# Loads of half a buffer, and two stores divided by rows into 112, 12 and 4, in an RMSNorm-matmul kernel

## The chip, the cores and the metric

The kernel runs on one core of one Trainium2 chip. The metric is the device time of one execution in microseconds (us), lower is better. A run counts as slow when it lies more than 1.5 per cent above the fastest run of the same kernel; verdicts use the others, the fast runs. The *span* of a profile is shorter than the time, by 1.8 us in the profiled run of the kernel before (208.8 and 210.53).

## The reference, cut to what matters

```python
# x [16, 1024, 512], gamma [512], weight [512, 768], all float32
rms = np.sqrt(np.mean(x ** 2, axis=-1, keepdims=True) + eps)
x_norm = x / rms * gamma
return np.matmul(x_norm, weight).astype(np.float32)      # [16, 1024, 768]
```

That is 16,384 tokens in 128 tiles of 128. The kernel reads 35 MB and writes 50 MB, so 85.5 MB have to pass through the DMA engines.

## The kernel before

A load brings 16 tiles: 128 rows, one for each partition of the on-chip memory, with 16 tokens of 2,048 B, that is 32,768 B a row. There are two such buffers. A store writes 8 tiles, 128 rows of 24,576 B, from one of three output buffers. All run on the sync engine's DMA queue. `XG` is 16, `OG` is 8, `NT` 128, `P` 128.

```python
    x_first, x_size = stretches(XG, {0: [2, 2, 4, 8], 1: [8, 8]})        # how each buffer is loaded
    o_first, o_size = stretches(OG, {0: [2, 2, 4], 1: [4, 4], last: [4, 4]})
    xin = ctx.enter_context(tc.tile_pool(name="xin", bufs=2))
    outp = ctx.enter_context(tc.tile_pool(name="out", bufs=3))
    ...
    def load(i):
        if i // XG not in x_tiles:
            x_tiles[i // XG] = xin.tile([P, XG, D], F32, name="xt")
        nc.sync.dma_start(out=held(x_tiles, XG, i, x_size[i]), in_=rows(x, i, x_size[i]))
    ...
    def store(i):
        first, n = o_first[i], o_size[i]
        if i == first + n - 1:
            nc.sync.dma_start(out=rows(out, first, n), in_=held(o_tiles, OG, first, n))
    ...
        marks = {NP - 10: (12, 13, 14, 15)}         # near the end: tiny loads of 12, 13, 14, 15 rows
        for j in range(1, NP):                      # a pair of tiles
            load_until(2 * j + AHEAD)
            ...                                     # GpSimd: cast to bf16; VectorE or TensorE: transpose
            for i, engine in ((2 * j, nc.scalar), (2 * j + 1, nc.vector)):
                a = accumulator()
                matmuls(i, a, range(K), feed)       # TensorE
                finish_tile(i, a, engine)           # scale by 1/rms into the output buffer, store
```

## Time and profile before

| | before |
|---|---|
| time, first three runs | 210.05, 210.16, 210.49 us |
| span of the profile | 208.8 us |
| TensorE busy | 195.0 us |
| bytes moved, rate over the span | 85.69 MB, 410 GB/s |
| last store: issued, first and last engine landed | 200.46, 206.46, 207.86 us |

The landings come from the steps of the DMA semaphores in the trace, one step read as one engine whose share has landed (a whole store shows 16 steps, the marks of 12 to 15 rows show 12 to 15). A *packet* is one row of a transfer on one DMA engine, 24,576 B in a whole store. The *granted clock* is the share of full speed that TensorE was given.

### The profile page before, as it was taken

The page shows a single profiled execution, that of the slowest core. Times are in us where ns is not written, and L with a number is a line of the kernel's source. Part 1 is how long each engine was busy: PE and PEld are TensorE (multiplying, and loading weights), DVE is VectorE, ACT ScalarE, POOL GpSimd, SP SyncE. Part 2 cuts the span into 40 slices and gives each one's busy share as a digit, 9 for nine tenths or more (in the row PEclk, how much of TensorE's full clock was granted, in tenths as well). Part 3 has the DMA queues.
Part 4 walks back from the last instruction along what each step waited for, and adds up shares of the span by engine and source line. Part 5 has one row for each costly group of instructions (what it writes and reads, how often), then busy time and mean ns, then how long its engine had stood idle before and what let it go on. Part 6 is the DMA issues. An engine that isn't in the chain of part 4 may idle for free.

```text
span 208.8 us, 3466 instructions
## 1 busy us (share of the span) xinstructions
PE 195.0 (93%) x1238; PEld 129.3 (62%) x1238; DVE 150.9 (72%) x270; ACT 149.6 (72%) x358; POOL 64.3 (31%) x65
## 2 busy tenths in 40 slices
PE   7799999999999999999999999999999989999910
PEld 2367767665677666666766666665667646666600
DVE  0465657997399957998499957998489955999410
ACT  4698787778677887788777877788678768778310
POOL 3247535003910193004810086001930049000000
PEclk9999999999999999999999999999999999999995
DMA  6999999999999999999999999999999999994994
GB/s 240 429 436 440 358 391 432 472 403 432 421 436 425 421 438 416 465 377 436 414 455 438 403 430 433 440 427 421 435 430 443 435 414 429 424 410 207 444 414 203
DMA packets 5025, 85.69 MB, mean 410 GB/s; under 512 B 654, under 2 KB 656, under 8 KB 1424
## 3 DMA queue, kind: packets, MB, share of 16 engines
q1 hardware_dynamic: 5004, 85.47, 96.7%
q8 instruction: 9, 0.15, 0.3%
q14 instruction: 8, 0.07, 0.1%
q10 hardware_dynamic: 4, 0.00, 0.0%
HBM read 35.14 MB, written 50.33 MB: 409 GB/s over the span
## 4 chain that ended last, share of the span: by engine, by line
PE 65%; DMA 25%; POOL 2%; DVE 1%; ACT 1%; SPq 1%; issue 1%; POOLq 0%
PE ops L194 56%; DMA xt<-in_x_dram 25%; PE tp L133 8%; POOL xb L94 2%; DVE ot L178 1%; ACT jk L98 1%; ACT ot L176 0%; SPq L232 0%; SPq L83 0%; SPq L191 0%; POOLq L94 0%; DVE xT L140 0%
## 5 line engine op out<-in xcount | busy, mean ns | idle before, releaser
L194 PE MATMUL ops<-w_bf,xT 128*128 128x512 bf16 (+1 forms) x800 | 147.5, 326 | 0.6 <-DVE w_bf L178 0.6
L194 PEld LDWEIGHTS <-xT 128*128 128x128 bf16 x800 | 78.3, 98 | 46.3 <-issue 0.8
L176 ACT ACTIVATE ot<-ops,rstd 128x768 f32<-128x768 f32 x64 | 57.7, 901 | 43.4 <-PE ops L194 43.0
L94 POOL CAST xb<-xt 128x1024 bf16<-128x1024 f32 (+1 forms) x52 | 51.1, 1012 | 108.5 <-DMA xt<-in_x_dram 89.0
L98 ACT ACTIVATE jk<-xt 128x512 bf16<-128x512 f32 x128 | 78.8, 619 | 2.1 <-DMA xt<-in_x_dram 2.1
L178 DVE TENSOR_SCALAR ot<-ops,rstd 128x768 f32<-128x768 f32 x64 | 64.6, 1009 | 9.5 <-PE ops L194 9.0
L133 PE MATMUL tp<-ident_f,xb 128*128 128x128 f32 x200 | 54.0, 274 | 2.6 <-POOL xb L94 2.6
L140 DVE COPY xT<-tp 128x1024 bf16<-128x1024 bf16 (+1 forms) x53 | 34.7, 656 | 27.1 <-PE tp L133 26.5
L172 DVE STREAM_TRANSPOSE xTq<-xq 32x256 f32<-32x256 f32 x112 | 48.8, 435 | 1.9
L194 PE MATMUL ops<-w_bf,xTq 128*128 128x512 bf16 x224 | 43.0, 326 | 0.0
L133 PEld LDWEIGHTS tp<-ident_f,xb 128*128 128x128 f32 x200 | 28.1, 141 | 7.5 <-POOL xb L94 5.2
L194 PEld LDWEIGHTS <-xTq 128*128 128x128 bf16 x224 | 22.2, 99 | 12.1
L98 ACT ACTIVATION_READ_ACCUMULATOR jk<-xt 128x1 f32 x128 | 24.4, 190 | 0.0
L158 POOL CAST xq<-xt 128x2048 bf16<-128x2048 f32 x7 | 13.3, 1899 | 4.2 <-DMA xt<-in_x_dram 4.2
L102 ACT ACTIVATE rms<-ssq,eps_sb 128x4 f32<-128x4 f32 (+1 forms) x35 | 10.4, 297 | 1.1
L104 DVE RECIPROCAL rstd<-rms 128x4 f32<-128x4 f32 (+1 forms) x35 | 6.1, 175 | 6.6 <-ACT rms L102 5.9
L253 PE MATMUL ops<-warm 128*128 128x512 bf16 x12 | 5.1, 577 | 1.2 <-DVE eps_sb L246 1.2
L253 PEld LDWEIGHTS <-warm 128*128 128x128 bf16 x12 | 1.4, 129 | 2.9 <-issue 1.7
L176 ACT ACTIVATE w_bf<-w_f,g_sb 128x768 bf16<-128x768 f32 x2 | 1.9, 934 | 1.3 <-DMA w_f<-in_weight_dram 1.3
L272 DVE COPY g_sb<-tp 128x4 f32<-128x4 f32 x1 | 0.2, 161 | 3.2 <-PE tp L270 3.2
L227 ACT ACT_TABLE_LOAD x1 | 1.3, 1283 | 1.3 <-PEq L343 1.3
L178 DVE TENSOR_SCALAR w_bf<-w_f,g_sb 128x512 bf16<-128x512 f32 (+2 forms) x3 | 1.4, 481 | 0.4 <-DMA w_f<-in_weight_dram 0.4
(10 smaller groups left out, 1.9 us busy)
## 6 DMA issues: line engine op xcount, KB each, us to landing
out_dram<-ot SPq DMA_DIRECT2D x13, 3072.0 KB, 18.1
xt<-in_x_dram SPq DMA_DIRECT2D x6, 4096.0 KB, 23.6
out_dram<-ot SPq DMA_DIRECT2D x5, 1536.0 KB, 11.6
xt<-in_x_dram SPq DMA_DIRECT2D x3, 2048.0 KB, 13.5
w_f<-in_weight_dram SPq DMA_DIRECT2D x2, 768.0 KB, 5.6
out_dram<-ot SPq DMA_DIRECT2D x2, 768.0 KB, 17.0
xt<-in_x_dram SPq DMA_DIRECT2D x2, 512.0 KB, 7.1
xt<-in_x_dram SPq DMA_DIRECT2D x1, 1024.0 KB, 9.1
```

The source lines that it names most:

```text
L94: engine.tensor_copy(out=xb_tiles[i // 2][:, i % 2:i % 2 + n, :], in_=held(x_tiles, XG, i, n))
L98: nc.scalar.activation(out=jk, in_=held(x_tiles, XG, i)[:, 0, :], func=AF.Square, accum_out=ssq)
L102: nc.scalar.activation(out=rms[:, :n], in_=ssq[:, :n], func=AF.Sqrt, scale=1.0 / D, bias=eps_sb)
L104: nc.vector.reciprocal(out=rstd[:, :n], in_=rms[:, :n])
L133: nc.tensor.transpose(out=tp_tiles[j][:, t, h, :], in_=words[:, lo:lo + P], identity=ident_f)
L140: nc.vector.tensor_copy(out=dst[:, t:t + n, :], in_=src[:, t:t + n, :])
L158: nc.gpsimd.tensor_copy(out=quads[q], in_=held(x_tiles, XG, 4 * q, 4))
L172: nc.vector.transpose(out=dst, in_=src)
L176: nc.scalar.mul(out=dst, in_=src, mul=r)
L178: nc.vector.tensor_single_scalar(out=dst, in_=src, scalar=r, op=mybir.AluOpType.mult)
L194: nc.tensor.matmul(out=acc[:, lo:hi], lhsT=xT_tiles[i // 2][:, i % 2, k // 2, :, k % 2], rhs=w_bf[:, k, lo:hi], start=(k == 0), stop=(k == ...
L253: nc.tensor.matmul(out=spare[:, :WIDE], lhsT=warm[:, :P], rhs=warm, start=True, stop=True)
```

## The change

The intent has two parts. The loads of tiles 64 to 127 come in eights, so that work on a buffer's first half can start before the second has landed. And two stores in the middle are divided so that the DMA engines that run late (the marks point to some of numbers 12 to 15) get fewer rows, and engines 0 to 3 more (rows an engine are estimates from the row counts). The last hunk of the edit issues both halves of a buffer at the turn at which the whole load was issued.

```diff
-    x_first, x_size = stretches(XG, {0: [2, 2, 4, 8], 1: [8, 8]})
+    x_first, x_size = stretches(XG, {0: [2, 2, 4, 8], **{g: [8, 8] for g in (1, 4, 5, 6, 7)}})
...
-            nc.sync.dma_start(out=rows(out, first, n), in_=held(o_tiles, OG, first, n))
+            cuts = [0, 112, 124, P] if first in (40, 48) else [0, P]
+            for lo, hi in zip(cuts, cuts[1:]):
+                nc.sync.dma_start(out=rows(out, first, n)[lo:hi], in_=held(o_tiles, OG, first, n)[lo:hi])
...
-            load_until(2 * j + AHEAD)
+            load_until((2 * j + AHEAD + XG - 1) // XG * XG)
```

## The prediction

> **What bounds the kernel now.** I read the page first: busy shares and the slices, then the waits of TensorE and of the DMA queue, then windows around the places where TensorE waits, and last the DMA packets and the semaphore steps of the landings, one by one.
>
> ```profile
> PE 195.0 (93%) x1238; PEld 129.3 (62%) x1238; DVE 150.9 (72%) x270; ACT 149.6 (72%) x358; POOL 64.3 (31%) x65
> ...
> DMA  6999999999999999999999999999999999994994
> ...
> q1 hardware_dynamic: 5004, 85.47, 96.7%
> ```
>
> Two things are full at once: TensorE at 93% and the DMA engines in nearly every slice. The one weak DMA slice is the 37th (187.9 to 193.1 us). So two chains have to be priced, and the later one counts.
>
> TensorE first. Its waits:
>
> ```profile
> PE tp L133 <- POOL xb L94: 2.6, 4, 0.9
> ...
> POOL xb L94 <- DMA xt<-in_x_dram: 89.0, 10, 16.3
> ```
>
> TensorE loses 2.6 us in four waits for a cast, and the cast waited for a load. The records put the four at 9.4 us (start-up), 50.7 (tile 32), 145.2 (tile 96) and 169.5 (tile 112). In the windows of 3 us around the last two (columns: time, then the busy us of each engine with its instructions, clock, DMA share, GB/s) the first number after the width, TensorE's busy time, should be 3.00:
>
> ```profile
> 119.60:122.60 3.00, 3.00 (x20) 1.73 (x19) 2.17 (x4) 2.52 (x7) 1.73 (x2) 1.00 1.01 429
> 143.60:146.60 3.00, 2.41 (x16) 1.33 (x14) 2.03 (x3) 2.48 (x7) 1.49 (x2) 1.00 1.03 442
> 168.00:171.00 3.00, 2.12 (x14) 1.14 (x13) 1.86 (x3) 2.31 (x6) 1.38 (x2) 1.00 0.95 410
> 187.00:191.00 4.00, 4.00 (x27) 2.52 (x26) 3.83 (x8) 3.14 (x7) 0.00 (x0) 1.00 0.32 135
> ```
>
> Start to start, the matmuls there lose 0.86 and 1.15 us beyond the usual 0.11, and 0.23 at 121.6: about 2.2 us in the part of the kernel that gets the smaller loads. The last row shows the other side: at 187 to 191 the DMA engines are only 0.32 busy, because the next store waits for TensorE.
>
> Now the DMA engines one by one. A load or store takes eight rows on each of 16 engines, and every engine adds one to the semaphore. Around 38 us the 16 landings of a store lie within 0.6 us, with one straggler (38.07 to 38.67, then 40.27). At 180 us they run from 179.85 to 185.36. The four little marks go to 12, 13, 14 and 15 rows; the landing each adds over the one before tells an engine: the 13th engine (number 12) 185.4, number 13 at 183.1, number 14 at 182.7. Another straggler, about 0.45 us behind number 12, is already among the first twelve; I call it X and cannot tell which it is. The last three stores end, typical engine and latest: 199.1 and 200.54, 202.8 and 204.20, 206.5 and 207.86. The latest engine finishes the store before at 193.03, then takes 7.51, 3.66 and 3.66 us, which is just the time of its rows (8 x 0.912 = 7.3; 8 x 0.460 = 3.7). **It never idles. The end of the kernel is the DMA queue of the slowest engine; the other engines idle at 191, most of them about 3 us.**
>
> [...] The trace agrees for the marks: 12, 13, 14 and 15 landings, each after one immediate step.
> [...] Now each engine runs at 24,576 B in 912 ns = 26.9 GB/s with 128-row transfers only; no run here shows fewer rows yet.
> [...] The trace agrees that such blocks exist: nine of 16,384 B, each taking about 0.9 to 1.1 us of some engine.[...]
>
> **The change part by part.**
> 1. Four 4 MB loads become eight of 2 MB. Bytes and issue place stay; the rounded bound issues both halves at the same turn as the whole one before. A row of 32,768 B takes 1213 ns, one of 16,384 B takes 611: 2 x 611 - 1213 = 9 ns a row, x 8 rows x 4 loads = 0.3 us more on every engine. What it wins: the first half lands some 8 x 0.61 = 4.9 us before the second, so the first cast of tiles 64, 80, 96, 112 no longer waits. The wide cast of the last four tiles waits for the second half, but TensorE needs the pair behind it three pairs (some 9 us) later. TensorE's chain gets up to 2.2 us shorter.
> 2. That gain meets the DMA tail. If TensorE ends at 197.2 in place of 199.4, typical engines could end about 204.3 instead of 206.5, but X has no idle time to give back: it still ends at 207.9 plus the 0.3 above.
> 3. The divided stores. A row is 8 tiles x 3,072 B = 24,576 B, 912 ns. Engines 0 to 3 get 7+1+1 = 9 rows, 4 to 11 get 8, 12 to 15 get 7. Over two stores: +1.82 us on engines 0 to 3, -1.82 on 12 to 15. Number 12, today about 0.4 behind at the end of the last store against X, is relieved; X is not. If X is one of 4 to 11, the end stays, 0.3 us later; if it is one of 0 to 3, it comes 1.8 + 0.3 = 2.1 later. An instruction block falling on another engine could help by about 1.
> 4. The cost that the row count hides. [...] the row takes up to 4 x 0.91 = 3.65 us on each, not 0.91, so +2.7 us per store on engines 0 to 11, and again +2.7 on engines 0 to 3 for the last piece. [...] Full lockstep would give 2 x 2.7 = 5.5 us on X if it is in 4 to 11 and 11 in 0 to 3; the engines are up to 4 us apart at that time, which takes off some[...]. Typical engines have about 3 us of idle time to swallow; X has none. My estimate for this case: the end 4 to 9 us later.
>
> **The rivals.** (a) *Only balance matters[...]*: the end moves by +0.3 (X in 4 to 11) to +2.1 us, so 210.4 to 212.3. [...] (b) [...] 214 to 219 us. [...] (c) *TensorE's waits were the bound*: then the smaller loads give 2.2 us, 208.0. Against it: the latest engine ran without a gap to the end. (d) A fresh TensorE wait because loads land late on engines 0 to 3: the half loads leave about 9 us for the second half, so at most 1 to 3 us, hidden behind (b).
>
> **Range and chances.** I give (b) a bit over half, (a) most of the rest, (c) or a lucky shift of instruction blocks little. The centre of (a) is 210.7, of (b) 216; weighted, about 213. Two per cent of 210.16 is 4.2 us, so slower means above 214.4: that is about three quarters of (b) plus a little. Faster by 2% would need 206.0. Even without any late engine, TensorE's end at 197.2, the last eviction (1.0), issue and landing (7.4), the end of the span after the last landing (0.9) and the 1.4 us between span and median time make 207.9: faster is nearly excluded. Range 209.0 to 219.0.
>
> **What would show it.** Step 1: no TensorE wait for the cast at tiles 96 and 112; landings of the halves about 5 us apart. Step 2: TensorE's last matmul near 197, the DMA engines hardly idle at 187 to 191. Step 3: the marks of number 12 to 14 about 2 us closer to the pack. Step 4: packets of 24,576 B during the stores of tiles 40 to 55 that take 1.8 to 3.6 us where nearly all took 0.91 to 0.97, and four engines late from then on. If those packets still take 0.91 us, step 4 is wrong and the time is 210 to 212. If X is relieved as well, the prediction is wrong towards 208.5.

The sum: without slow pieces, case (a), +0.3 to +2.1 us; with slow small pieces, case (b), the end 4 to 9 us later, put at 214 to 219 us; weighted, about 213. The terms of (b): the slow rows of the small pieces (2 x 2.7 = 5.5 us, or 11); the term for the 112-row pieces, "some" without a number. The factor of four in the 2.7 was in no trace read by then; e15 measured it later: 4.83 and 4.88 us a packet for 4 and 12 neighbouring rows stored alone on the queue, 1.22 for all 128.

Engine numbers are names by the marks: number 12 is the engine that the mark on 13 rows adds, and so on. In the trace of before, each mark from 13 rows on shows every landing of the mark before again, 0.15 to 0.21 us later, and one more. In that of the changed kernel the pieces of a divided store show 16, 12 and 4 landings. That rows are shared out evenly (eight an engine for 128: the latest engine's 7.51 us is near 8 x 0.912), and that small pieces go to the same engines as marks of few rows, is the author's estimate: the records do not name the engine. The nine packets of 16,384 B are those of the queue that the page calls "q8 instruction" (879 to 1094 ns each).

## More of the kernel before

From the profile page of the kernel before: the span, the rate in 40 equal slices, and the chain that ended last as shares of the span by engine (the other lines that matter are in the prediction).

```profile
span 208.8 us, 3466 instructions
...
GB/s 240 429 436 440 358 391 432 472 403 432 421 436 425 421 438 416 465 377 436 414 455 438 403 430 433 440 427 421 435 430 443 435 414 429 424 410 207 444 414 203
...
PE 65%; DMA 25%; POOL 2%; DVE 1%; ACT 1%; SPq 1%; issue 1%; POOLq 0%
```

The rate stays at 377 GB/s or above from the sixth slice to the 36th, and the chain changes back and forth between TensorE (PE) and the DMA.

## The result, and the profile after

| | before | after |
|---|---|---|
| median of 6 runs | 210.39 us | 218.7 us |
| all 6 runs | 210.05 to 210.49 | 215.14 to 221.33 |
| fast runs | all | 215.14, 216.42, 216.85, 217.21 (a seventh run counted) |
| ratio of fast runs | 1 | 1.0289 (95%: 1.0249 to 1.0330) |
| span of the profile (fast) | 208.8 | 213.3 |

A ratio here is the mean time of one kernel's fast runs over that of the other's of the same rounds, so it is not quite the ratio of the medians above. In fast runs the change costs 2.9 per cent, 6.1 us; the median of all runs is 8.3 us higher, because three of its six runs fell above the 1.5 per cent line and are left out of the ratio. The changed kernel also scatters: 6 us between its runs where the kernel before has 0.4.

From the page of the changed kernel, the lines that answer to those of before:

```profile
span 213.3 us, 3484 instructions
PE 194.9 (91%) x1238; PEld 129.4 (61%) x1238; DVE 151.2 (71%) x270; ACT 148.9 (70%) x358; POOL 64.3 (30%) x65
...
DMA  6999999999999999999999999999999999987993
GB/s 255 424 446 427 316 423 433 456 400 448 422 438 418 423 438 406 441 439 346 317 310 383 389 443 436 419 429 430 433 438 406 443 439 424 423 379 333 433 424 143
...
q1 hardware_dynamic: 5612, 85.47, 97.0%
...
PE 50%; DMA 40%; DVE 1%; POOL 1%; issue 1%; ACT 1%; SPq 1%; POOLq 0%; ACTq 0%
```

TensorE has the same work. The bytes are the same. The DMA engines are busy in the same tenths up to the end, but slices 19 to 23 (96 to 123 us) move 310 to 389 GB/s instead of 403 to 455: **the engines are busy and move less**. A busy share alone hides this; the rate shows it. The same in windows (columns: time, width, then busy us of TensorE with its instructions, its weight loads, VectorE, ScalarE, GpSimd, granted clock, DMA share, GB/s), first before, then after:

```profile
93.00:117.00 24.00, 24.00 (x158) 16.23 (x157) 19.83 (x35) 18.75 (x47) 7.87 (x7) 1.00 1.01 434
117.00:141.00 24.00, 24.00 (x156) 16.09 (x155) 19.62 (x36) 18.53 (x47) 7.87 (x7) 1.00 1.00 430
```

```profile
93.00:117.00 24.00, 24.00 (x158) 16.33 (x157) 19.81 (x36) 18.73 (x47) 6.00 (x6) 1.00 1.00 351
117.00:141.00 24.00, 21.59 (x140) 14.29 (x138) 17.04 (x31) 16.59 (x43) 7.86 (x7) 1.00 1.00 420
```

While the divided stores run, the rate falls from 434 to 351 GB/s and TensorE does not notice. It pays in the next window: 2.4 us without a matmul. The waits of the changed kernel say why:

```profile
ACT ot L176 <- DMA out_dram<-ot: 10.7, 3, 4.0
...
DVE ot L178 <- DMA out_dram<-ot: 3.6, 3, 1.6
...
PE tp L133 <- POOL xb L94: 2.8, 3, 1.1
PE ops L196 <- ACT ot L176: 2.8, 3, 1.4
```

The first two and the last are new. A late store holds one of the three output buffers, so ScalarE and VectorE cannot write their next tile (14.3 us of waiting in all), the accumulators stay full, and TensorE waits for ScalarE (at 134, 159 and 183 us). The old wait for a cast is no smaller in sum (2.8 us after 2.6): the ones at tiles 96 and 112 are gone, but the one at tile 32 is longer, and one of 1.1 us has come at tile 80, whose load landed late.

The landings of the first and the last of the 16 engines, from the semaphore steps (for the divided stores, the 112 rows' first and the 4 rows' last):

```
                         before            after
load up to tile 79       92.6 to  96.5     92.6 to  96.1
store of tiles 48 to 55 107.2 to 111.1    107.6 to 116.6
load up to tile 95      116.9 to 120.7    117.5 to 127.2
store of tiles 104-111  187.2 to 193.0    188.9 to 197.9
last store              206.5 to 207.9    209.6 to 212.4
```

The last engine loses 6.5 us between 96 and 127 us and ends 4.5 us later. And the packets: of 1664 packets of 24,576 B, those that took over 1.5 us were 0 before and 51 after; the longest took 1.37 and 3.55 us.

### The profile page after: what moved, and what is told of

Its sections match the earlier page's. It is cut to its first block, busy times and chain, and to the rows that moved or that the text cites. A ratio compares the mean times of both kernels' runs of the same rounds, so it can differ in the third digit from the quotient of the medians.

```text
span 213.3 us, 3484 instructions
## 1 busy us (share of the span) xinstructions
PE 194.9 (91%) x1238; PEld 129.4 (61%) x1238; DVE 151.2 (71%) x270; ACT 148.9 (70%) x358; POOL 64.3 (30%) x65
## 4 chain that ended last, share of the span: by engine, by line
PE 50%; DMA 40%; DVE 1%; POOL 1%; issue 1%; ACT 1%; SPq 1%; POOLq 0%; ACTq 0%
PE ops L196 44%; DMA out_dram<-ot 26%; DMA xt<-in_x_dram 13%; PE tp L133 6%; DVE ot L178 1%; POOL xb L94 1%; ACT ot L176 1%; SPq L234 0%; SPq L83 0%; SPq L193 0%; DVE xT L140 0%; POOLq L94 0%; ACTq L176 0%
```

## The experiments

The theory: a DMA that has only some of the 128 rows, neighbouring ones above all, moves its bytes more slowly than one of all 128. Its rivals: only the row balance counts; the smaller loads cost it; more DMAs cost it. All edits are to the kernel before unless said otherwise. All outputs were right except in e13. e6, e7 and e15 ran once each, for their traces; their state is unknown.

### e1: the loads in eights alone

```diff
+ the first and the last hunk of the change; stores whole
```

> Only the loads of tiles 64 to 127 in eights, stores whole. Theory [...]: nothing slow is left, 208.5 to 210.8 us; the TensorE waits for the cast at tiles 96 and 112 are gone; the packets of 24,576 B take 0.91 to 0.97 us again; the end stays with the slowest DMA engine, so little or nothing is won. Rival (the smaller loads themselves or their issue cost the time): 213 us or more.

Measured: 210.43 us median, ratio 1.0011 (0.9996 to 1.0026). TensorE's waits, the window of the two stores, and the window at 187 to 191:

```profile
PE tp L133 <- POOL xb L94: 1.5, 2, 0.8
...
93.00:117.00 24.00, 23.84 (x155) 16.28 (x156) 19.80 (x36) 18.74 (x48) 7.49 (x7) 1.00 1.00 429
187.00:191.00 4.00, 4.00 (x26) 2.44 (x25) 3.87 (x7) 3.57 (x11) 0.00 (x0) 1.00 0.70 295
```

The two whole stores run at the rate of before (429 and 434 GB/s). The waits at tiles 96 and 112 are gone; what is left is at 9.4 and 50.7 us. TensorE is ahead: the last store is issued at 198.78 instead of 200.46 us, and the DMA engines are 0.70 busy at 187 to 191 where they were 0.32. The last store's first engine lands at 204.76 instead of 206.46, its last at 207.46 instead of 207.86. So 1.7 us were won on TensorE and on the typical engine, and nearly nothing on the one that sets the end. The eights are innocent of the loss, and gain nothing by themselves.

### e2: the divided stores alone

```diff
+ the middle hunk of the change; loads as before
```

> Only the stores of tiles 40 to 55 divided into 112, 12 and 4 rows, loads as before. Theory [...]: 214 to 219 us in fast runs, packets of 24,576 B of 1.6 to 3.6 us between 93 and 117 us, and later loads and stores landing late on some engines. Rival (only the balance of rows between engines counts): 210.4 to 212.3 us with all packets at 0.91 to 0.97 us.

Measured: 218.78 us median (216.37 to 221.34), ratio of the fast runs 1.0369 (1.0303 to 1.0434). Of 1664 packets, 61 took over 1.5 us; this profile is of a slow run (221.34 us), and the fast one of the same kernel in e12 has 50. The divided stores make the whole loss; plain row balance (210.4 to 212.3 us) is out.

### e3: 112 and 16 rows, so that no engine gets more

```diff
-            cuts = [0, 112, 124, P] ...          # of the change
+            cuts = [0, 112, P] ...               # 7 + 1 rows an engine, by the row count
```

> The same two stores divided into 112 and 16 rows: 7 and 1 rows on each of the 16 engines, so no engine gets more or less than before. Theory [...]: slower by 4 to 10 us, 214 to 220 us. Rival of balance: no change, 210.0 to 210.8 us.

Measured: 218.64 us median, ratio 1.0382 (1.0351 to 1.0413). By the row count (7 + 1 for 8, an estimate) every engine moves what it moved before, and the loss is as large. It isn't imbalance.

### e4: as many DMAs, cut along the tiles

```diff
+            cuts = [0, 6, 7, 8] if first in (40, 48) else [0, n]
+            for lo, hi in zip(cuts, cuts[1:]):
+                nc.sync.dma_start(out=rows(out, first, n)[:, lo:hi], in_=held(o_tiles, OG, first, n)[:, lo:hi])
```

> The same two stores in three pieces each, but cut along the tiles (6, 1 and 1 tiles of all 128 rows): as many DMAs as in the change[...]. Theory [...]: within 0.5 per cent of before, 209.6 to 211.2 us. Rival (more DMAs, semaphores and descriptors cost it): 213 us or more.

Measured: 210.95 us median, ratio 1.0036 (1.0020 to 1.0051). The window of the two stores in e3, then in e4:

```profile
93.00:117.00 24.00, 23.84 (x155) 16.27 (x156) 19.81 (x36) 18.75 (x47) 7.86 (x7) 1.00 1.00 336
```

```profile
93.00:117.00 24.00, 23.84 (x155) 16.24 (x156) 19.80 (x36) 18.71 (x47) 7.86 (x7) 1.00 1.01 423
```

Three DMAs for each store cost 0.4 per cent when each has all 128 rows; two cost 3.8 per cent when they are cut by rows. The number of DMAs is not the cause; which rows one DMA has is.

### e5 and e8: 64 and 64, 96 and 32 rows

```diff
+            cuts = [0, 64, P] ...                # e5
+            cuts = [0, 96, P] ...                # e8
```

> The two stores divided into 64 and 64 rows, loads as before: 4 and 4 rows on each of the 16 engines, no engine gets more, only two DMAs. Theory [...]: each half at up to half the rate, so up to 7.3 us more per store in lockstep, less because engines drift into the other half: 214 to 224 us, packets of 24,576 B bunched near 1.8 us. Rival (it was only the very small pieces of 4 and 12 rows): at most 0.5 per cent slower, 210 to 211.3 us.

> The two stores divided into 96 and 32 rows: 6 and 2 rows on each of the 16 engines[...]. Theory [...]: milder than 112 and 16[...]: 212.5 to 218 us, packets near 1.8 us more than near 3.6 us. Rival (any division by rows costs the same[...]): as the 112 and 16 division, 217 to 220 us.

Measured: e5 222.13 us median, ratio 1.0542 (1.0478 to 1.0605); e8 218.94 us, ratio 1.0388 (1.0334 to 1.0442). The window of e5:

```profile
93.00:117.00 24.00, 24.00 (x157) 16.30 (x156) 19.81 (x36) 18.74 (x47) 7.85 (x7) 1.00 1.02 300
```

e5 has no small piece, two DMAs, equal shares by the row count, and is the worst of the stores: 116 packets over 1.5 us, the rate at 300 GB/s. So small size isn't the cause. For e8 I had expected something milder than e3; it is the same within the error. A second piece of 32 rows for 16 did not help. The first piece changed too, so this alone does not tell the two apart; e13 and e14 do.

### e13 and e14: which piece costs it

```diff
+            hi = 112 if first in (40, 48) else P                       # e13: rows 112 to 127 never stored
+            nc.sync.dma_start(out=rows(out, first, n)[:hi], in_=held(o_tiles, OG, first, n)[:hi])
```

```diff
+            if first in (40, 48):                                      # e14: beside the whole store
+                nc.sync.dma_start(out=spare_rows[:, :n], in_=held(o_tiles, OG, first, n)[112:])
```

> Wrong on purpose: of the two stores only rows 0 to 111 are written, in one DMA each, the 16 rows left are never stored. So the few-row pieces are gone and only the big piece off the 16 x 8 pattern stays; every engine has 0.9 us less to move per store. If the big piece causes most of the loss: 213 to 217 us, packets near 1.8 us. If the few-row pieces cause it: 208 to 210.4 us.

> The stores whole as before, and beside the two of them rows 112 to 127 stored once more, to a scratch tensor (outputs right): the few-row piece alone[...]. The extra bytes alone are 2 x 0.91 = 1.8 us an engine. If the few-row piece costs as much [...] (3.65 us a row): up to 7.3 us, 214 to 218 us. If the big piece is the main cost: 212 to 213 us.

Measured: e13 214.88 us median, ratio 1.0200 (1.0178 to 1.0222), that is 4.2 us slower (clear of noise, though the interval straddles 2 per cent) although each engine, by the row count, moves 2 x 0.91 = 1.8 us less; so about 6.0 us of harm. e14 218.56 us median, ratio 1.0362 (1.0303 to 1.0421), that is 7.6 us slower with 1.8 us more to move; about 5.8 us of harm. Packets of 24,576 B, from the packet records (the profile of e14 is of a slow run, 220.91 us, and there is no fast one):

```
                      all run: over 1.5 us   longest   93 to 118 us: mean
before                          0             1.37           0.92 us
the change                     51             3.55           1.18
e3  112 and 16                 67             5.26           1.25
e5  64 and 64                 116             2.24           1.39
e13 112 rows only              42             3.74           1.16
e14 whole, and 16 more         42             4.91           1.25
```

Both pieces are harmful, and counted by the engines' bytes each about as much as the other. Counted by what sixteen neighbouring rows took alone in e15, four times the usual (4.85 against 1.22 us), the two pieces that e14 adds come to 2 x 4 x 0.91 = 7.3 us (an estimate), nearly all of its 7.6. By bytes, the two kinds of piece do not add up (6.0 and 5.8 alone, 6 to 8 together); why is not shown by a run.

### e6 and e15: a transfer alone on the queue

A tail after the kernel loads rows of x into the on-chip memory and stores them from there into a scratch tensor, each transfer waiting for the one before. e6 uses rows of 12,288 B, e15 of 32,768 B.

```diff
+        for sel in (slice(0, P), slice(124, 128), slice(0, 16, 4), slice(112, 124), slice(112, 128), slice(0, 128, 8), slice(0, 112), slice(0, 64)):
+            nc.sync.dma_start(out=tail, in_=whole)
+            nc.sync.dma_start(out=tail[sel], in_=whole[sel])
+            nc.sync.dma_start(out=spare_rows[sel], in_=tail[sel])
```

> The kernel before with a tail that moves rows of 12,288 B alone on the queue, first loads into the on-chip memory, then stores from it to a scratch tensor (outputs unchanged; the total time grows by some 100 us and says nothing). Per packet[...]: whole 128 rows 0.46 us; rows 124 to 127 1.84 us; four rows four apart 0.46; rows 112 to 123 1.84; rows 112 to 127 1.84; every eighth row [...] 0.92; rows 0 to 111 between 0.46 and 0.92. [...] Rival [...]: 0.46 to 0.5 everywhere.

> The tail run again with rows of 32,768 B (alone 1.21 us), because the division of loads cost 17 us where the tail with 12,288 B had shown loads unharmed. [...] a load's packets 3.5 to 4.9 us for 4, 12 and 16 neighbouring rows and near 1.2 for 4 rows four apart, about 2.4 for every eighth row and for much of the 64 and 112 rows. [...] 1.2 to 1.6 us everywhere, and the loss of the divided loads has another cause. Stores: 4.3, 1.2, 4.3, 4.3, 2.1 us as the shorter rows showed, scaled. The total time says nothing.

(The first list of each is what the theory gives, in e15 for loads; 0.46 to 0.5 and 1.2 to 1.6 us everywhere are the other case.)

Measured in e15 (median time of a packet; rate is bytes over the time from the first packet's start to the last one's end):

```
rows                load: us, GB/s     store: us, GB/s
0 to 127             1.21   391         1.22   424
124 to 127           3.64    34         4.83    26
0, 4, 8, 12          1.99    62         1.22   102
112 to 123           3.61    92         4.88    76
112 to 127           3.68   121         4.85   101
every eighth         2.30   178         2.40   200
0 to 63              2.57   194         2.56   202
0 to 111             2.04   245         1.23   310
```

For stores this is the theory in plain numbers: a packet of four, twelve or sixteen neighbouring rows takes four times as long as one of all 128 (4.83, 4.88 and 4.85 against 1.22 us), and the rates, 26, 76 and 101 GB/s, are 25 to 26 for every four of these. Four spaced rows run at full speed (1.22 us, 102 GB/s). Sixteen rows eight apart and 64 neighbours take twice as long (2.40 and 2.56 us, 200 and 202 GB/s). What in the chip sets these steps is not shown. The rows are chosen alike in the on-chip memory and in the chip's main memory, so the two sides were not varied apart; but the length of the stretch written there does not explain the rates: twelve neighbouring rows of 12,288 B (147 KB) were stored at 74 GB/s in e6, four of 32,768 B (131 KB) at 26 in e15. The last line is the large piece of the change: 310 GB/s are left of 424. In proportion to its rows it would have 112/128 of 424, or 371 (an estimate; 64 rows kept nearly their half). Where the rest goes is not shown: the records do not name the engine.

Loads show the same, less cleanly. e6 had borne out the stores (1.62 us for four neighbouring rows, 0.46 for four spaced ones, 0.80 for every eighth), but had misled me about loads: there the load of four neighbouring rows took 0.61 us and that of four spaced rows 0.60 (whole: 0.46), and I read it as loads being free. In e15 it is 3.64 against 1.99 us. Its rows are longer, but they also lie closer in main memory (32,768 B apart, 262,144 in e6), so which of the two makes the difference is open. Why four spaced rows load at 1.99 and not 1.21 us isn't explained.

### e9 and e10: the same balance by dividing loads

```diff
+        cuts = [0, 112, 124, P] if i in (64, 80) else [0, P]                 # e9, loads of 16 tiles
+        cuts = [0, 112, 116, 120, 124, P] if i in (72,) else [0, P]          # e10, with the eights
+        for lo, hi in zip(cuts, cuts[1:]):
+            nc.sync.dma_start(out=held(x_tiles, XG, i, x_size[i])[lo:hi], in_=rows(x, i, x_size[i])[lo:hi])
```

> The kernel before with the same division into 112, 12 and 4 rows made in two loads (tiles 64 to 79 and 80 to 95, rows of 32,768 B) and not in stores. Theory ([...] as the tail run measured: 1.63 against 0.46 us for a store's row, 0.61 against 0.60 for a load's): little harm, 210 to 212.5 us, the end set by engine 4, whose share is unchanged. Rival (any division by rows off the 16 x 8 pattern costs the same in either direction): 216 us or more.

> The loads in eights, and the load of tiles 72 to 79 divided into 112 rows and four times 4 rows: engines 4 to 15 carry 7 rows of 16,384 B, engines 0 to 3 eleven; so engine 4 and engine 12, the late ones, give up 0.61 us each. Theory (the end is the queue of the slowest DMA engine): 0.3 to 0.6 us faster than before, 209.7 to 210.1 us. Rival (TensorE or something else sets the end): 210.4 us as with the eights alone; or slower [...]: 211 us or more.

Measured: e9 228.12 us median, ratio 1.0821 (1.0789 to 1.0853); e10 215.04 us, ratio 1.0216 (1.0191 to 1.0240). The theory's forecast failed in both, for the inference from e6; the rivals named beside it (216 us or more, 211 us or more) came true. In e9 (one wait and one window of its trace):

```profile
PE tp L135 <- POOL xb L96: 17.5, 4, 9.1
...
84.00:102.00 18.00, 14.57 (x94) 9.41 (x92) 14.14 (x25) 10.67 (x26) 0.00 (x0) 0.97 1.02 230
```

The packets of the first divided load took 2.2 to 2.4 us in the median (1.21 whole), those of its small pieces about 3.2, and the rate fell to 230 GB/s. A late load is on TensorE's path at once, so it lost 17.5 us waiting for casts. e10, one load of half the size divided, lost 4.6 us, where it should have won 0.3 to 0.6: no version with a division by rows beats the kernel before.

### e7: which engine is late

```diff
-        marks = {NP - 10: (12, 13, 14, 15)}
+        marks = {NP - 10: (1, 2, 3, 4, 5, 6, 7, 8, 9, 10, 11, 12)}
```

> The kernel before with marks on 1 to 12 rows instead of 12 to 15: each mark adds the landing of one more engine, so the number of the late engine X shows. If X is one of 4 to 11 (72 per cent likely to me), the row balance of the change would leave it as it was; if it is one of 0 to 3, the change would make it 1.8 us later. Time 210 to 211 us.

Measured: the last landings of the marks on 1, 2, 3, 4 and 5 rows were 180.20, 181.49, 181.66, 182.39 and 185.26 us. The fifth engine, number 4, is the late one in this run, and so very likely X; the store before had its two last landings at 184.91 and 185.08. It is outside 0 to 3, so the division, by the row count, left its share as it was, and could not shorten its queue. The time, 213.9 us, was wrongly expected: so many marks made the sync queue wait, and the next store was issued at 186.94 us instead of 178.09.

```profile
SPq L265 <- DMA out_dram<-ot: 12.6, 2, 7.4
```

### e11 and e12: are the eights of use beside the divided stores?

The changed kernel and e2 once more, in the same rounds.

> The changed kernel again, on the same chip and in the same rounds as the divided stores with the old loads, to see what the eights are worth beside the divided stores. Theory: the eights take away TensorE's wait of 8 us for the late load of tile 80, and the DMA queues then set the end: 215 to 217.5 us in fast runs, 1 to 3 us less than the divided stores with whole loads. Rival: the eights are worth nothing here either, both 216 to 219 us.

> The divided stores with the loads of before, beside the changed kernel: 216 to 219 us in fast runs, a TensorE wait of some 8 us near tile 80. Rival: as the changed kernel within 0.5 us.

Measured: the changed kernel 217.72 us median (216.34 to 223.59), ratio 1.0320 (1.0277 to 1.0362); the divided stores with old loads 220.85 us (216.40 to 222.10), of which only the 216.40 counts as fast, so there is no ratio. Inconclusive as a time. The fast profiles tell the difference in kind. Divided stores with old loads:

```profile
PE tp L133 <- POOL xb L94: 7.4, 2, 6.9
...
117.00:141.00 24.00, 17.05 (x99) 10.82 (x98) 11.15 (x20) 11.59 (x28) 7.86 (x7) 0.86 1.01 422
```

The changed kernel, second profile:

```profile
PE tp L133 <- POOL xb L94: 4.7, 2, 4.0
...
117.00:141.00 24.00, 19.82 (x109) 12.32 (x108) 12.77 (x24) 13.08 (x31) 7.91 (x7) 0.86 1.00 419
```

With whole loads TensorE waits 6.9 us for the load that starts at tile 80; with eights 4.0 here, and 1.1 in the first profile. With the two longer waits the granted clock was 0.86 in this window (1.00 in the first profile): the clock records show half speed from 125.6 to 132.5 us, though the wait of 6.9 us ended at 128.7, and from 124.7 to 131.5, though the wait of 4.0 ended at 125.5. So in these two runs matmul speed was lost on top of the wait; that the wait was the cause is not shown. The same program gave waits of 1.1 and 4.0 us, so what the divided stores do to the queue differs from run to run. That fits the scatter of the changed kernel, but no run shows that it is all of it.

## Why the prediction was right or wrong, point by point

**What bounds the kernel: right.** e1 took away TensorE's two waits of the second half, and the time stayed (1.0011), because the last engine's queue did not get shorter.

**Part 1, the eights: right in size.** The forecast was up to 2.2 us on TensorE; the last store was issued 1.7 us earlier in e1.

**Part 2, the gain meets the tail: right.** First landing 1.7 us earlier, last 0.4.

**Part 3, the row balance: right where it could be tested, of no weight.** X is very likely engine 4 (e7), among the 4 to 11 that keep their share. That numbers 12 to 14 would come closer to the pack was half right: in the changed kernel 13 (about 185.4) and 14 (about 184.7) landed their marks early, but number 12 was still among the last (190.7, of a field from 183.8 to 190.7).

**Part 4, the slow pieces: the size was right; of the mechanism only the effect is shown** (for stores alone on the queue by e15, 4.83 and 4.88 against 1.22 us; that the same slowness binds in the full queue is argued from e3, e4, e5, e13 and e14). The forecast for this case alone was 4 to 9 us; fast runs lost 6.1. The sign it named came too: 30 packets of 1.8 to 3.6 us at 93 to 118 us. The few-row term, 2.7 us a store, was about right (5.8 for two stores in e14, 2.9 each). But one term was mis-sized: the 112-row piece was to add "some". e13, with this piece alone, is 4.2 us slower outright, 6.0 by the bytes.

**The step that failed is the weighing.** "I give (b) a bit over half, (a) most of the rest": so a centre of 216 was pulled down to 213, a change of 2.8 us where 6.1 was measured in fast runs and 8.3 between the medians. Rival (a) rested on one sentence, an assumption that no trace shows. The trace of before could not speak against (a), since but for the tiny marks it holds 128-row transfers only. e3 does: with equal shares, where (a) allows next to nothing, the loss is 3.8 per cent, 8.0 us. What is left to learn is that a mean between two cases is a value that neither of them gives.

**Rival (d) was sized on the small side.** "At most 1 to 3 us, hidden behind (b)": in the changed kernel TensorE waited 1.1 and 4.0 us for the late load in the two profiles. And one wait was not on the list at all: stores that land late hold the output buffers (14.3 us of waiting by ScalarE and VectorE, 2.8 us by TensorE). With whole loads the wait is 6.9 us, so the eights shortened this wait; whether they saved time beside the divided stores is not shown.

**The scatter was not foreseen.** The kernel before repeats within 0.5 per cent; this one does not.

**A slip without effect.** The 1.4 us from span to time set the span of one run against the median of others. In the profiled run it is 1.8, so the floor without any late engine was 208.3 us and not 207.9.

## What to carry to other kernels

Cut a DMA along the bytes of a row, not by rows: a transfer of all 128 rows kept its rate when it was cut into three along the tiles (423 and 434 GB/s, 0.4 per cent), and any cut by rows, made in two stores or in one or two loads, cost 2 to 8 per cent here, equal shares or not. When DMA engines are always busy, look at the rate beside the busy share: 434 against 351 GB/s at the same share was what gave it away. And before giving the slowest engine less work, find out which one it is; a few tiny transfers on 1, 2, 3 ... rows tell it (in e7 the last landing was 182.39 us with four rows, 185.26 with five), as long as they don't hold up the queue.
